# Sample states from two row groups of 32 tokens, state space states behind the first recurrence head, first evacuations on VectorE

## The chip, the cores and the metric

The kernel runs on one core of one Trainium2 chip. The metric is the time of one execution on the device in microseconds (us), as the median of several runs. In the profile the engines are called PE (TensorE, matrix products), DVE (VectorE), ACT (ScalarE), POOL (GpSimd) and SP (SyncE, which issues most DMA transfers).

## The reference

One inference step of a two-layer hybrid decoder. A prompt of 512 tokens and a sample group of 8 sequences of 8 tokens use the same weights; the model width is 1024. Layer 0 mixes tokens with 4 mLSTM heads and 4 retention heads, layer 1 with 4 HGRN2 heads (`hgrn`) and an S5 state space model. Behind each mixer come a squared-ReLU MLP and a gated per-layer embedding. Everything is fp32.

```python
# per layer i
hn = rmsnorm(h, norm_mix[i])
out, *st = ab_mixer(hn, ...) if i % 2 == 0 else cd_mixer(hn, ...)
h = h + out
hn = rmsnorm(h, norm_ff[i])
h = h + square(relu(hn @ w_ff1[i])) @ w_ff2[i]
gate = sigmoid(rmsnorm(h, norm_ple[i]) @ w_ple_gate[i])
h = h + gate * (p[i] @ w_ple_proj[i])
```

Each head of the three recurrences also returns its new state of 128 x 128 (mLSTM: 128 x 129 with the normaliser) for each of the 8 sample sequences, for instance for HGRN2:

```python
S = exp(b_last)[..., None] * S + einsum('bhsk,bhsv->bhkv', kc * exp(b_last[:, :, None] - b), vc)
```

Over the 64 sample tokens this is, for each sequence b, the product of the keys and the values of b's 8 tokens, added to the decayed old state.

## The kernel before

All 576 tokens (512 of the prompt, 64 samples) are one tile of 128 x 576. A projection is made a column at a time: 128 outputs by 576 tokens, from 8 blocks of 128 inputs. For fp32 accuracy weights and activations are split in a high and a low part, and a block is three products (`mm3`, L240 to L247), each in two halves of 288 tokens: 48 products on L245 for a column. The weight's high part is made by ACT (L233) and the low part by DVE or POOL (L234). A column collects in a buffer `pb` in PSUM, which an engine evacuates. Small products go to other PSUM buffers, `pm`. Where the pools are set by `psum(3)` there are three `pb` buffers and two `pm`; with `psum(2)` two and four.

The program runs `load` (the inputs, and the layer 0 embedding projection), the first mixer with mLSTM heads and retention heads, the MLP, the embedding, the second mixer, MLP, embedding, and the final norm. A scheduler sets each engine's order of instructions from the order of the program, a priority (`high_priority`) and the dependencies; an engine then runs its list strictly in that order, and so does SP with its DMAs.

Three places matter here.

`load` (L358 to L383). Two embedding tiles `pin` and the hidden state `h` of 8 tiles are loaded over SP, and eight columns of the embedding are computed. Each is evacuated to `po` with factor 0.5 by ACT (L380), and a DMA queue of POOL stores `po` to DRAM; `po` has three buffers. A copy of one column of `pin` to h[0] (L369) makes the load of h[0] wait until that copy is done, so SP issues it last of the eight.

`state_out` (L747 to L764) is called once for each of the 12 heads, for the sample sequences. POOL spreads the values of the 64 tokens to `Vm`, where the columns of sequence b keep only the rows of its tokens (a mask from `vmask`, L756), for three, three and two sequences. A PE product on L758 with the 64 tokens as its rows contracts the keys `Kt` with it, 384, 384 and 256 columns (387, 387 and 258 with the normaliser), and DVE adds each result to the state `s_in` (L761 or L763). The sample outputs of a head come from `s_in` and `qd` on L778 just before, in products that fill 32 columns of the PE array.

The second mixer (L1465 to L1490): four columns `su` of the state space model, then `s5_state` (L1203 to L1249) for four groups of channels `ct`: tables `sR` and `sE` from DRAM into five shared buffers, two groups of four products on L1220, and nine DVE instructions (L1226 to L1234, one of them a scan, L1230) that run the recurrence. Then `hgrn` (L1300) for heads 0 to 3, each with columns f, q, i and g (evacuations on L1313, L1334, L1337, L1340), a scan over tokens (L1329), exponent factors `e` (L1385, L1387) for a hierarchy of small products on PE (L1373, L1408), and its state. The outputs of the state space model are made after head 1.

Of the kernel before, what the change touches and what calls it, by code (L numbers as in the profile page):

```python
# [16 lines left out]
P = 128  # L17
NP = 512
NS = 64
# [28 lines left out]

def c0_layout():
    cols, n = {}, 0  # L50
    for name, w in (("ident", 128), ("qmask", 128), ("vmask", 8), ("m01", NT), ("negp", 128), ("negs", 64),
                    ("sel", 512), ("cos", NT), ("sin", NT), ("rdec", 512), ("rdecs", 256),
                    ("rint", 512), ("rints", 256), ("rkd", 4), ("rkds", 4)):
        cols[name] = (n, n + w)
        n += w
    return cols, n
# [7 lines left out]
def const0():  # L64
# [14 lines left out]
    qm = np.zeros((NB, NS), np.float32)  # L79
    qm[s // 8, s] = 1.0  # L80
    put("qmask", np.broadcast_to(qm[:4, :32].reshape(1, -1), (P, 128)))
    put("vmask", qm.T)
    sel = np.zeros((36, 4, P), np.float32)
    for h in range(4):
        sel[h, h] = 1.0
# [85 lines left out]
class K:  # L171
# [188 lines left out]
    def load(self):  # L360

        nc = self.nc
        with self.tc.tile_pool(name="lp", bufs=2) as lp:
            with self.tc.high_priority(60):
                raw = self.fetch("col2", "w_ple_proj", 0, 0, 0)
                pin = self.embed_in(0, lp, nc.sync)
                ws = [self.parts(raw)]

                nc.vector.tensor_copy(self.h[0][:, 0:1], pin[1][:, 0:1])  # L369
            for k in range(KD):  # L370
                nc.sync.dma_start(self.h[k], self.A["hT"][k])
                if k == 3:
                    ws.append(self.unit("col2", "w_ple_proj", 0, 512, 0))
            nc.sync.dma_start(self.cc, self.A["c0"][:, :NCC])
            for n2 in range(2):
                for n in range(4):
                    ps = self.cols(ws[n2], self.xple, (2 * n, 2 * n + 1))
                    o = lp.tile([P, NT], F32, name="po", tag="po", bufs=3)
                    with self.tc.high_priority(60):
                        nc.scalar.mul(self.sv(o), self.pv(ps), 0.5)  # L380
                    nc.gpsimd.dma_start(self.prd[n2 * 4 + n], o)
                if n2 == 0:
                    self.gate_w = self.unit("gate")  # L383
# [363 lines left out]
    def state_out(self, name, h, n, C, Kt, V, dec, hp):  # L747

        nc = self.nc
        Cn = C  # L750
        if dec is not None and not isinstance(dec, float):
            nc.gpsimd.tensor_tensor(Cn, C, dec.unsqueeze(2).to_broadcast([P, NB, n]), ALU.mult)
        for b0, b1 in ((0, 3), (3, 6), (6, 8)):
            ps = self.pmt()[:, :(b1 - b0) * n]
            Vm = hp.tile([NS, 3, n], F32, name="Vm", tag="Vm", bufs=2)[:, :b1 - b0]
            nc.gpsimd.tensor_tensor(Vm, V[:NS, 4, :n].unsqueeze(1).to_broadcast([NS, b1 - b0, n]),  # L756
                                    self.vmask[:, b0:b1].unsqueeze(2).to_broadcast([NS, b1 - b0, n]), ALU.mult)
            nc.tensor.matmul(ps, Kt[:NS, 4], Vm.rearrange("p b n -> p (b n)"), start=True, stop=True)  # L758
            o = Cn[:, b0:b1].rearrange("p b n -> p (b n)")
            if isinstance(dec, float):  # L760
                nc.vector.scalar_tensor_tensor(o, C[:, b0:b1].rearrange("p b n -> p (b n)"), dec, ps, ALU.mult, ALU.add)  # L761
            else:
                nc.vector.tensor_tensor(o, o, ps, ALU.add)  # L763
        nc.sync.dma_start(self.A[name][h], Cn)  # L764

    def qdiag(self, q, hp, tag="qd"):

# [694 lines left out]
    def mix1(self):  # L1462
        nc, tc = self.nc, self.tc
        with ExitStack() as st:
# [8 lines left out]
            with self.psum(3):  # L1473
                self.s5_in(xs, r, sp)
                r = r()
            st.enter_context(self.psum(2))
            self.s5_state(sp)
            self.hgrn(0, xs, r, hp)
            self.hgrn(1, xs, r, hp)
            self.s5_out(sp, range(4))  # L1480
            self.hgrn(2, xs, r, hp)
# [119 lines left out]
```

## Time and profile before

| | |
|---|---|
| median of 3 runs | 1675.05 us (1671.84 to 1675.14) |
| the profiled execution | 1673.67 us, span of the instructions 1671.9 us |
| PE busy | 1599.5 us, 96% of the span |
| DVE busy | 994.9 us, 60% |
| ACT busy | 619.5 us, 37% |
| POOL busy | 244.9 us, 15% |
| mean granted clock of PE | 0.979 |

The profile is of one execution. A busy time is the sum of an engine's instruction times, which can overlap with those of other engines; the span is from the first to the last instruction. The chain of waits follows the work that ended last back to what released it. The granted clock is a share of the full 2.4 GHz: 0.5 is the 1.2 GHz level, and a value between them is a mean over a stretch that has both.

### The profile page before, as it was taken

To read this page: it belongs to the slowest core of one execution; us is meant where nothing else is said; L and a number is where in the kernel's file an instruction comes from. 1 tells how busy PE (TensorE), PEld (TensorE's weight loads), DVE (VectorE), ACT (ScalarE), POOL (GpSimd) and SP (SyncE) were. 2 spreads that over 40 slices of the span, in tenths; PEclk is the share of its full clock that TensorE was granted. 3 is DMA by queue.
4 is the path that set the end of the run, shared out by engine and by line. 5 is a ranking of instruction groups with operands and counts; after the bars stand their busy time and mean duration, and the time that the engine had idled before them with its cause. 6 is when DMAs were issued, how large, how long until landed. Compare 5 with 4: busy or idle time off the path is not lost.

```text
span 1671.9 us, 30272 instructions
## 1 busy us (share of the span) xinstructions
PE 1599.5 (96%) x12613; PEld 1549.1 (93%) x12613; DVE 994.9 (60%) x1830; ACT 619.5 (37%) x1016; POOL 244.9 (15%) x236
## 2 busy tenths in 40 slices
PE   6999999999999999999999788989999999999996
PEld 6999799999999999999998778879999999999995
DVE  4987665658954636347666796386633424334365
ACT  5333222335313223144542356463522413224353
POOL 1321232301000000001023465241000000000100
PEclk8999999999999999999999889999999999999998
DMA  6322222223332323324436322522222222222221
GB/s 251 110 91 81 93 78 102 78 75 103 115 116 78 121 87 116 108 80 141 146 104 192 114 76 82 147 77 78 77 89 85 80 89 76 89 89 91 89 89 57
DMA packets 77226, 168.81 MB, mean 101 GB/s; under 512 B 29216, under 2 KB 34208, under 8 KB 76960
## 3 DMA queue, kind: packets, MB, share of 16 engines
q1 hardware_dynamic: 75432, 163.40, 28.9%
q8 instruction: 99, 1.62, 0.4%
q0 software_dynamic: 640, 2.36, 0.4%
q10 hardware_dynamic: 1016, 1.11, 0.2%
q14 instruction: 39, 0.32, 0.1%
HBM read 142.70 MB, written 24.13 MB: 100 GB/s over the span
## 4 chain that ended last, share of the span: by engine, by line
PE 85%; DVE 7%; ACT 3%; DMA 2%; issue 2%; SPq 1%; DVEq 0%; ACTq 0%
PE pb L245 77%; PE pm L758 2%; PE pm L528 1%; PE pm L778 1%; DVE e L1385 1%; PE pm L870 1%; SPq L1270 1%; DMA s5U<-yd 0%; SPq L1201 0%; ACT wh L233 0%; PE pm L795 0%; DVE s5w L1230 0%; ACT xh L280 0%; PE pm L872 0%; DVE h L429 0%
## 5 line engine op out<-in xcount | busy, mean ns | idle before, releaser
L245 PE MATMUL pb<-xh,wh 128*128 128x288 f32 x2480 | 548.6, 300 | 34.2 <-ACT po L380 7.2
L245 PE MATMUL pb<-xl,wh 128*128 128x288 f32 x2480 | 546.9, 299 | 0.0
L245 PE MATMUL pb<-xh,wl 128*128 128x288 f32 x2480 | 546.5, 299 | 0.0
L233 ACT CAST wh<-wr 128x1024 fp32r<-128x1024 f32 x219 | 229.7, 1049 | 745.2 <-PE pb L245 672.9
L245 PEld LDWEIGHTS pb<-xh,wh 128*128 128x128 f32 x2480 | 406.0, 191 | 44.1 <-issue 12.5
L245 PEld LDWEIGHTS pb<-xl,wh 128*128 128x128 f32 x2480 | 407.1, 191 | 5.7 <-issue 5.4
L245 PEld LDWEIGHTS pb<-xh,wl 128*128 128x128 f32 x2480 | 407.0, 191 | 4.0 <-issue 3.2
L234 DVE TENSOR_TENSOR wl<-wr,wh 128x1024 fp32r<-128x1024 f32 x199 | 246.2, 1238 | 24.6 <-ACT wh L233 16.0
L245 PE MATMUL pb<-uh,wl 128*128 128x288 f32 x1024 | 219.2, 296 | 0.0
L245 PE MATMUL pb<-ul,wh 128*128 128x288 f32 x1024 | 218.8, 295 | 0.0
L245 PE MATMUL pb<-uh,wh 128*128 128x288 f32 x1024 | 218.8, 295 | 0.0
L458 DVE TENSOR_TENSOR h<-h,pb 128x576 f32<-128x576 f32 x64 | 48.2, 754 | 210.8 <-PE pb L245 210.8
L245 PEld LDWEIGHTS pb<-uh,wl 128*128 128x128 f32 x1024 | 163.9, 188 | 0.6 <-DVE s5R L951 0.4
L245 PEld LDWEIGHTS pb<-uh,wh 128*128 128x128 f32 x1024 | 163.8, 188 | 0.6 <-issue 0.6
L245 PEld LDWEIGHTS pb<-ul,wh 128*128 128x128 f32 x1024 | 164.2, 188 | 0.0
L322 POOL TENSOR_TENSOR sqa<-sqa,sq 128x576 f32<-128x576 f32 x20 | 33.0, 1648 | 876.2 <-ACT sq L321 876.2
L445 DVE SCALAR_TENSOR_TENSOR fu<-pb,r 128x576 f32<-128x576 f32 x64 | 48.3, 756 | 179.4 <-PE pb L245 179.3
L234 POOL TENSOR_TENSOR wl<-wr,wh 128x1024 fp32r<-128x1024 f32 x20 | 50.8, 2543 | 103.6 <-ACT wh L233 102.0
L278 DVE TENSOR_TENSOR ul<-fu,uh 128x576 fp32r<-128x576 f32 x64 | 48.3, 755 | 9.5 <-ACT uh L277 9.3
L756 POOL TENSOR_TENSOR Vm<-V,cc 64x384 f32<-64x384 f32 (+3 forms) x36 | 32.0, 900 | 103.1 <-ACT V L740 63.8
L446 ACT ACTIVATE fu<-fu 128x576 f32<-128x576 f32 x64 | 43.8, 686 | 8.5 <-DVE fu L445 8.2
L281 DVE SCALAR_TENSOR_TENSOR xl<-h,vec,xh 128x576 fp32r<-128x576 f32 x48 | 39.7, 837 | 11.8 <-ACT xh L280 11.8
(459 smaller groups left out, 1506.9 us busy)
## 6 DMA issues: line engine op xcount, KB each, us to landing
wr<-in_w_dram SPq DMA_DIRECT2D x219, 512.0 KB, 3.2
sR<-Rd SPq DMA_DIRECT2D x12, 256.0 KB, 3.8
h<-in_hT_dram SPq DMA_DIRECT2D x8, 288.0 KB, 5.3
prd<-po POOLq DMA_DIRECT2D x8, 288.0 KB, 5.9
Gd<-s5G SPq DMA_DIRECT2D x4, 576.0 KB, 3.9
prj<-prd SPq DMA_DIRECT2D x8, 288.0 KB, 6.0
sG<-Gd SPq DMA_DIRECT2D x8, 288.0 KB, 5.0
s_in<-in_Cst_dram SPq DMA_DIRECT2D x4, 516.0 KB, 7.4
```

Of the source, the lines that this page charges most:

```text
L233: nc.scalar.copy(hi, raw)
L234: (nc.gpsimd if self.lo_pool else nc.vector).tensor_tensor(lo, raw, hi.bitcast(F32), ALU.subtract)
L245: mm(ps[:, j if bank is None else bank, :HALF], a, b[:, j * HALF:(j + 1) * HALF], start=first and a is wh and b is xh, stop=last and a is wl)
L278: nc.vector.tensor_tensor(lo, src, hi.bitcast(F32), ALU.subtract)
L281: nc.vector.scalar_tensor_tensor(lo, src, scale, hi.bitcast(F32), ALU.mult, ALU.subtract)
L322: (nc.vector if i or dve else nc.gpsimd).tensor_tensor(acc[i], acc[i], t, ALU.add)
L445: nc.vector.scalar_tensor_tensor(self.sv(u), self.pv(ps), 0.0, self.sv(r()), ALU.max, ALU.mult)
L446: nc.scalar.activation(u, u, AF.Square)
L458: nc.vector.tensor_tensor(self.sv(self.h[n]), self.sv(self.h[n]), self.pv(ps), ALU.add)
L528: nc.tensor.transpose(dst, src[:n, t0:t0 + tn], self.ident[:n, :n])
L756: nc.gpsimd.tensor_tensor(Vm, V[:NS, 4, :n].unsqueeze(1).to_broadcast([NS, b1 - b0, n]), self.vmask[:, b0:b1].unsqueeze(2).to_broadcast([N ...
L758: nc.tensor.matmul(ps, Kt[:NS, 4], Vm.rearrange("p b n -> p (b n)"), start=True, stop=True)
```

## The change

In `load` the copy to h[0] goes away, and the eight evacuations go from ACT to DVE. In `state_out` the 64 tokens are taken as two row groups, rows 0 to 31 with sequences 0 to 3 and rows 32 to 63 with sequences 4 to 7. A folded mask (four more columns of `vmask`) lets one POOL product serve both, with four blocks of 128 columns; two PE products follow, each with 32 rows and 512 columns, into two PSUM buffers. For mLSTM a third PE product with the mask itself as its 8 columns gives the normaliser. In the second mixer head 0 is called before `s5_state`.

```diff
@@ c0_layout
-    for name, w in (("ident", 128), ("qmask", 128), ("vmask", 8), ("m01", NT), ("negp", 128), ("negs", 64),
+    for name, w in (("ident", 128), ("qmask", 128), ("vmask", 12), ("m01", NT), ("negp", 128), ("negs", 64),
...
-    put("vmask", qm.T)
+    put("vmask", np.concatenate([qm.T, qm[:4].T + qm[4:].T], 1))
@@ load
-                pin = self.embed_in(0, lp, nc.sync)
+                self.embed_in(0, lp, nc.sync)
                 ws = [self.parts(raw)]
-
-                nc.vector.tensor_copy(self.h[0][:, 0:1], pin[1][:, 0:1])
...
-                        nc.scalar.mul(self.sv(o), self.pv(ps), 0.5)
+                        nc.vector.tensor_scalar(self.sv(o), self.pv(ps), 0.5, None, ALU.mult)
@@ state_out
-        Cn = C
-        if dec is not None and not isinstance(dec, float):
-            nc.gpsimd.tensor_tensor(Cn, C, dec.unsqueeze(2).to_broadcast([P, NB, n]), ALU.mult)
-        for b0, b1 in ((0, 3), (3, 6), (6, 8)):
-            ps = self.pmt()[:, :(b1 - b0) * n]
-            Vm = hp.tile([NS, 3, n], F32, name="Vm", tag="Vm", bufs=2)[:, :b1 - b0]
-            nc.gpsimd.tensor_tensor(Vm, V[:NS, 4, :n].unsqueeze(1).to_broadcast([NS, b1 - b0, n]),
-                                    self.vmask[:, b0:b1].unsqueeze(2).to_broadcast([NS, b1 - b0, n]), ALU.mult)
-            nc.tensor.matmul(ps, Kt[:NS, 4], Vm.rearrange("p b n -> p (b n)"), start=True, stop=True)
-            o = Cn[:, b0:b1].rearrange("p b n -> p (b n)")
...
+        Vm = hp.tile([NS, 4, P], F32, name="Vm", tag="Vm", bufs=2)
+        nc.gpsimd.tensor_tensor(Vm, V[:NS, 4, :P].unsqueeze(1).to_broadcast([NS, 4, P]),
+                                self.vmask[:, 8:].unsqueeze(2).to_broadcast([NS, 4, P]), ALU.mult)
+        ps = [self.pmt() for _ in range(2)]
+        rows = [slice(32 * g, 32 * g + 32) for g in range(2)]
+        for g in range(2):
+            nc.tensor.matmul(ps[g], Kt[rows[g], 4], Vm[rows[g]].rearrange("p b n -> p (b n)"), start=True, stop=True)
+        if n > P:
+            pn = self.pmt()[:, :8]
+            nc.tensor.matmul(pn, Kt[:NS, 4], self.vmask[:, :8], start=True, stop=True)
+        for g in range(2):
+            add(C[:, 4 * g:4 * g + 4, :P], ps[g].rearrange("p (b n) -> p b n", b=4))
+        if n > P:
+            add(C[:, :, P], pn)
@@ the second mixer
+            self.hgrn(0, xs, r, hp)
             self.s5_state(sp)
-            self.hgrn(0, xs, r, hp)
             self.hgrn(1, xs, r, hp)
```

The following rows are the instructions as they stand in an engine's list: line, operation, output and inputs with buffer numbers, shape, and how many stand together. First PE, before, at the state products of the first retention head (`s_in` and `qd` are the sample state and query, `pb` a projection column):

```order
L870 MATMUL pm_2588<-V_2537,W_2557 128x128
L872 MATMUL pm_2588<-Cs_2570,qi_2567 128x128
L778 MATMUL pm_2589<-s_in_2581,qd_2583 32x128 x8
L758 MATMUL pm_2608<-Vm_2609,Kt_2547 128x384
L758 MATMUL pm_2613<-Vm_2614,Kt_2547 128x384
L245 MATMUL pb_2664<-xl_368,wh_2660 128x288
```

The third product, L758 with 256 columns, stood 12 rows further down, between column products. The same place on PE after the change:

```order
L878 MATMUL pm_2571<-V_2520,W_2540 128x128
L880 MATMUL pm_2571<-Cs_2553,qi_2550 128x128
L786 MATMUL pm_2572<-s_in_2564,qd_2566 32x128 x8
L764 MATMUL pm_2593<-Vm_2591,Kt_2530 128x512
L764 MATMUL pm_2594<-Vm_2591,Kt_2530 128x512
L245 MATMUL pb_2640<-xl_367,wh_2636 128x288
```

Three products became two, which are neighbours here, and the third place among the columns is gone. Next DVE, before, at the start of the second mixer: the last evacuation of a state space column (`su`), the first channel group's recurrence (`s5w`, `s5Z`), and head 0's f column (`z`, from `pb_10000`):

```order
L1197 TENSOR_TENSOR su_9823<-pb_9774,r_9468 128x8x8
L1226 TENSOR_TENSOR s5w1_9869<-s5Z_9538,sR_9845 64x512
L1227 TENSOR_TENSOR s5w1_9869<-s5Z_9538,sR_9845 64x512
L1228 TENSOR_TENSOR s5w0_9868<-s5Z_9538,sR_9844 128x512
L1229 TENSOR_TENSOR s5w0_9868<-s5w0_9868,s5w1_9869 128x512
L1230 SCALAR_TENSOR_TENSOR s5w0_9868<-sR_9846,s5w0_9868 128x512
L1231 TENSOR_TENSOR s5w1_9869<-s5w0_9868,sR_9845 64x512
L1232 TENSOR_TENSOR s5w1_9869<-s5w0_9868,sR_9845 64x512
L1233 TENSOR_TENSOR s5w0_9868<-s5w0_9868,sR_9844 128x512
L1313 TENSOR_TENSOR z_10049<-pb_10000,r_9468 128x576
```

In the changed kernel DVE goes from the same evacuation to head 0, and its first recurrence instruction stands behind the second half of head 0's output `mo`, 76 instructions on:

```order
L1205 TENSOR_TENSOR su_9778<-pb_9729,r_9423 128x8x8
L1321 TENSOR_TENSOR z_9854<-pb_9805,r_9423 128x576
L1325 TENSOR_SCALAR z_9854<-z_9854 128x576
...
L809 SCALAR_TENSOR_TENSOR mo_10337<-pm_10331,gnh_82,gT_10042 128x64
L1234 TENSOR_TENSOR s5w1_10365<-s5Z_9493,sR_10341 64x512
L1235 TENSOR_TENSOR s5w1_10365<-s5Z_9493,sR_10341 64x512
```

The recurrence moved from ahead of head 0 to the middle of head 1. Further on in the same list, on DVE after the change, the fourth group's recurrence and head 2's f column (`z_11262`) stand among head 1's level work (`Wc`, `e`):

```order
L1236 TENSOR_TENSOR s5w0_10469<-s5Z_9493,sR_10445 128x512
L1321 TENSOR_TENSOR z_11262<-pb_11213,r_9423 128x576
L1237 TENSOR_TENSOR s5w0_10469<-s5w0_10469,s5w1_10470 128x512
L1384 COPY_PREDICATED Wc_10768<-lev_84,pm_10771 128x128
L1385 COPY_PREDICATED Wc_10768<-lev_84,pm_10771 64x32
L1393 TENSOR_TENSOR e_10891<-b_10560 128x144x2
L1238 SCALAR_TENSOR_TENSOR s5w0_10469<-sR_10447,s5w0_10469 128x512
```

Before, head 0's f column stood so among the first groups. In `load` DVE's list gains the evacuations `po`; after the change, from the split of h[3] to that of h[4] (`xl` is a low part, `sqa` the sum of squares of the norm):

```order
L281 SCALAR_TENSOR_TENSOR xl_348<-h3_124,vec_70,xh_347 128x576
L322 TENSOR_TENSOR sqa_326<-sqa_326,sq_351 128x576
L378 TENSOR_SCALAR po_184<-pb_171 128x576
L234 TENSOR_TENSOR wl_163<-wr1_160,wh_162 128x1024
L378 TENSOR_SCALAR po_200<-pb_187 128x576
L378 TENSOR_SCALAR po_216<-pb_203 128x576
L281 SCALAR_TENSOR_TENSOR xl_355<-h4_125,vec_70,xh_354 128x576
```

Here the first three evacuations stand between two splits; before, DVE ran the splits of h[2] to h[7] in a row with none between them.

## Rows read from the trace of the kernel before

**Rows 1.** The page, part 1: busy us of each engine (share) xinstructions.
```profile
PE 1599.5 (96%) x12613; PEld 1549.1 (93%) x12613; DVE 994.9 (60%) x1830; ACT 619.5 (37%) x1016; POOL 244.9 (15%) x236
```

**Rows 2.** The page, part 4: the chain that ended last, by engine, by line.
```profile
PE 85%; DVE 7%; ACT 3%; DMA 2%; issue 2%; SPq 1%; DVEq 0%; ACTq 0%
PE pb L245 77%; PE pm L758 2%; PE pm L528 1%; PE pm L778 1%; DVE e L1385 1%; PE pm L870 1%; SPq L1270 1%; DMA s5U<-yd 0%; SPq L1201 0%; ACT wh L233 0%; PE pm L795 0%; DVE s5w L1230 0%; ACT xh L280 0%; PE pm L872 0%; DVE h L429 0%
```

**Rows 3.** Busy time by stretch: us, busy by engine, PEclk, DMA share, GB/s.
```profile
350.00:840.00 490.00, 489.06 (x3694) 484.07 (x3694) 295.30 (x632) 173.02 (x240) 18.20 (x15) 1.00 0.33 109
892.00:1012.00 120.00, 101.05 (x1015) 94.40 (x1016) 95.47 (x127) 54.51 (x103) 60.22 (x47) 0.87 0.36 116
```

**Rows 4.** The same by stretch, of the column products on L245 alone.
```profile
350.00:840.00 490.00, 481.71 (x3585) 477.79 (x3585) 1.00 0.33 109
892.00:1012.00 120.00, 75.51 (x488) 72.35 (x489) 0.87 0.36 116
```

**Rows 5.** The same by stretch, of the recurrence's tile s5w alone (DVE).
```profile
892.00:1012.00 120.00, 38.99 (x36) 0.87 0.36 116
```

**Rows 6.** The same by stretch, of the state space products on L1220 alone.
```profile
892.00:1012.00 120.00, 9.25 (x64) 8.58 (x64) 0.87 0.36 116
```

**Rows 7.** PE's waits from 850 to 1180: us in total, times, longest.
```profile
PE pb L245 <- DVE z L1337: 6.3, 1, 6.3
PE pm L1220 <- DMA sE<-Ed: 6.3, 4, 3.2
PE pb L245 <- DVE gT L1340: 5.2, 1, 5.2
```

**Rows 8.** Timeline of DVE from 918 to 937: start, us, instruction.
```profile
927.52 3.25 DVE L1230 TENSOR_TENSOR_SCAN s5w<-sR,s5w 128x512 f32<-128x512 f32 x1
930.70 2.49 DVE L1387 TENSOR_TENSOR e<-e,q 128x256 f32<-128x256 f32 x1
933.11 0.74 DVE L1337 TENSOR_TENSOR z<-pb,r 128x576 f32<-128x576 f32 x1
...
934.21 0.69 DVE L1231 TENSOR_TENSOR s5w<-s5w,sR 64x512 f32<-64x512 f32 x1
```

**Rows 9.** Costliest groups, DVE from 892 to 1012: xcount | busy, mean ns.
```profile
L1230 DVE TENSOR_TENSOR_SCAN s5w<-sR,s5w 128x512 f32<-128x512 f32 x4 | 6.9, 1728 | 0.1
```

**Rows 10.** Busy time by stretch of 6 us, columns as in rows 3.
```profile
924.00:930.00 6.00, 3.70 (x28) 3.47 (x26) 5.90 (x4) 3.65 (x5) 6.00 (x4) 1.00 0.00 0
930.00:936.00 6.00, 1.30 (x4) 0.98 (x4) 5.92 (x8) 0.00 (x0) 2.90 (x1) 0.67 0.16 44
936.00:942.00 6.00, 3.55 (x16) 3.58 (x17) 3.39 (x7) 1.14 (x3) 0.00 (x0) 0.50 0.56 187
```

**Rows 11.** Timeline of PE from 234 to 241, the first retention head's state.
```profile
234.44 1.07 PE L778 MATMUL pm<-s_in,qd 128*32 128x128 f32 x16
235.44 1.55 PE L758 MATMUL pm<-Vm,Kt 64*128 64x384 f32 x4
236.93 0.40 PE L245 MATMUL pb<-xl,wh 128*128 128x288 f32 x1
...
239.78 0.70 PE L758 MATMUL pm<-Vm,Kt 64*128 64x256 f32 x2
240.41 0.40 PE L245 MATMUL pb<-xh,wl 128*128 128x288 f32 x1
```

**Rows 12.** Timeline of PE from 5 to 45, idle before and its releaser in brackets.
```profile
23.01 0.85 PE L245 MATMUL pb<-xh,wh 128*128 128x288 f32 x2 [5.04 <-ACT po L380]
30.63 0.59 PE L245 MATMUL pb<-xh,wh 128*128 128x288 f32 x2 [2.15 <-ACT po L380]
```

**Rows 13.** Timeline of DVE from 6 to 45, the splits of h.
```profile
17.37 4.46 DVE L281 SCALAR_TENSOR_TENSOR xl<-h,vec,xh 128x576 fp32r<-128x576 f32 x6
```

**Rows 14.** Timeline of ACT from 18 to 42, one of the eight evacuations.
```profile
27.79 0.65 ACT L380 ACTIVATE po<-pb 128x576 f32<-128x576 f32 x1 [2.62 <-DMA prd<-po]
```

**Rows 15.** The page, part 5: an evacuation of a column on DVE.
```profile
L445 DVE SCALAR_TENSOR_TENSOR fu<-pb,r 128x576 f32<-128x576 f32 x64 | 48.3, 756 | 179.4 <-PE pb L245 179.3
```

More of the change, by code (lines that the diff above doesn't have):

```diff
@@ L749, in state_out, with add @@
         nc = self.nc
-        Cn = C
-        if dec is not None and not isinstance(dec, float):
-            nc.gpsimd.tensor_tensor(Cn, C, dec.unsqueeze(2).to_broadcast([P, NB, n]), ALU.mult)
-        for b0, b1 in ((0, 3), (3, 6), (6, 8)):
-            ps = self.pmt()[:, :(b1 - b0) * n]
-            Vm = hp.tile([NS, 3, n], F32, name="Vm", tag="Vm", bufs=2)[:, :b1 - b0]
-            nc.gpsimd.tensor_tensor(Vm, V[:NS, 4, :n].unsqueeze(1).to_broadcast([NS, b1 - b0, n]),
-                                    self.vmask[:, b0:b1].unsqueeze(2).to_broadcast([NS, b1 - b0, n]), ALU.mult)
-            nc.tensor.matmul(ps, Kt[:NS, 4], Vm.rearrange("p b n -> p (b n)"), start=True, stop=True)
-            o = Cn[:, b0:b1].rearrange("p b n -> p (b n)")
+        if not isinstance(dec, float):
+            nc.gpsimd.tensor_tensor(C, C, dec.unsqueeze(2).to_broadcast([P, NB, n]), ALU.mult)
+        def add(o, ps):
             if isinstance(dec, float):
-                nc.vector.scalar_tensor_tensor(o, C[:, b0:b1].rearrange("p b n -> p (b n)"), dec, ps, ALU.mult, ALU.add)
+                nc.vector.scalar_tensor_tensor(o, o, dec, ps, ALU.mult, ALU.add)
             else:
                 nc.vector.tensor_tensor(o, o, ps, ALU.add)
-        nc.sync.dma_start(self.A[name][h], Cn)
+        Vm = hp.tile([NS, 4, P], F32, name="Vm", tag="Vm", bufs=2)
[12 more added lines that the diff above has]
+            add(C[:, :, P], pn)
+        nc.sync.dma_start(self.A[name][h], C)
     def qdiag(self, q, hp, tag="qd"):
```

## The prediction

> **What bounds the kernel now.** I read the page's busy table and chain first, then the busy time by stage, then the waits, and last the timelines of the stages that the change touches. PE is busy 1599.5 of 1671.9 us [rows 1], and the chain that ended last is PE for 85%, 77% of it the column products of L245 [rows 2]. So a saving counts only if it shortens PE's own work or an idle stretch of PE. The table by stage shows where PE is not full: from 350 to 840 us it is busy 489.06 of 490 at full clock, while from 892 to 1012, the start of the second mixer, it is busy 101.05 of 120 and the granted clock averages 0.87 [rows 3]. Here DVE is busy 95.47 of 120, and 38.99 of that are the 36 instructions of the state space recurrence [rows 3, 5]: nine for each of four groups of channels. In the waits of this stage PE's longest ends at z of head 0 (6.3 us) and another at gT (5.2) [rows 7]. DVE's timeline shows why: recurrence instructions, with a scan of 3.25 us, are queued ahead of z at 933.11, although the column of z was done by then [rows 8]. PE stood idle, the clock then fell to 0.67 and to 0.50 in the next slices [rows 10], that is partly and then wholly to the 1.2 GHz level after the idle time.
>
> The profiled execution took 1673.67 us, 1.8 more than its span, and the median of the runs is 1675.05. I make the sum as differences and take them from the median.
>
> **Part 1, state space behind head 0 (C).** First the present loss. Idle time is 120 - 101.05 = 18.95 us [rows 3]. The 488 column records took 75.51 us here, 0.1547 each, against 481.71/3585 = 0.1344 at full clock [rows 4]: 488 x 0.0203 = 9.9 us of slow clock. Together 28.9 us. The same slowdown on the small products of head 0 is not in it; with it the clock's share is at most 0.13 x 120 = 15.6, so 34.6 is the upper bound.
>
> In the new order PE goes from the state space columns straight to f, q, i and g of head 0, and DVE has z, the scan, e and gT of head 0 with no recurrence ahead of them. A column is 48 products of 0.1344 us, 6.45 us, so PE has 4 x 6.45 = 25.8 us, and part of head 1's first column, to cover head 0's chain on DVE. Some waits inside a head's levels (e, Wc, W) belong to any head and remain; I leave 5 us with their clock.
>
> The recurrence now stands behind mo of head 0. Its DVE work is unchanged: 39.0 us, plus three evacuations of about 0.75 us among it, about 41 us, before z of head 2, which holds a PSUM buffer. PE's cover there: the eight groups of L1220, 9.25 us [rows 6], and by the order the remaining 33 of 48 products of head 1's g column and three columns of head 2, 3.7 x 6.45 = 23.9, together 33 us. The shortfall is 41 - 33 = 8 us of idle, with the clock behind it (9.9 per 18.95 us of idle above, about half as much again) 12 us. If DVE runs the chain undisturbed it is much shorter: a 64x512 product of it takes 0.69 us at 934.21 [rows 8], where POOL has gone quiet [rows 10], so eight of the nine instructions at 0.69 and a scan at the mean of four, 1.73 [rows 9], make 7.25 a group, 29 in all, plus 2, which 33 us would cover: loss 0. POOL still makes the low parts of some weights in this stage, as it did beside the 3.25 us scan, when it was busy for 6.00 of 6 us [rows 10], so I stay nearer the contended end: 9 us. After: 5 + 9 = 14 us against 28.9, **C = 15 us**. Bounds: 28.9 - 27 = 2 if the stretch behind head 0 loses nearly as much as the present one, 34.6 - 5 = 29 if it loses nothing.
>
> A wait that moves: each group's tables arrive in five shared buffers, freed by the group before. PE waited 6.3 us in four such waits [rows 7]. They stay and are now queued in PE ahead of head 1's levels; that is in the 9. On SP the weight loads behind those table loads wait with them; the columns of head 2 are there by my walk. Head 2 onwards has the same order as before, so a lead gained here is kept.
>
> The Trainium skill (SBUF — State Buffer, "SBUF: two separate sides") says that a DVE instruction with two SBUF inputs and a GpSimd instruction that reads SBUF exclude each other for a whole instruction. The 3.25 us scan beside a busy POOL agrees [rows 8, 10]. By that rule the contended 41 us hold and C is 28.9 - 5 - 12 = 12; without it, 24.
>
> **Part 2, state products in two row groups (B).** In the first retention head two 384-column products take PE from 235.44 to 236.93, 1.48 us, and the third, of 256 columns among column products, from 239.78 to 240.41, 0.63 us [rows 11]. With a price a per column and s per entry into this shape, 768a + s = 1.48 and 256a + s = 0.63: a = 1.66 ns, s = 0.205 us. One 512-column product then costs 0.85. No trace of before has two row groups, so the pair is bounded: side by side 0.85 + 0.2 = 1.05, one after the other 1.70 + 0.2 = 1.90, against 2.11 now. The nearest row for the choice is that of the eight 128-column products (16 records) just before, which go to two column groups: 1.07 us [rows 11], less 0.2 for the entry 0.87, where one by one at 1.66 ns a column they would take 8 x 128 x 1.66 = 1.70. They overlap two deep, so I take 1.05.
>
> By the order the two products are neighbours in the last mLSTM head, all four retention heads and hgrn heads 0, 2 and 3; in mLSTM heads 0 to 2 and hgrn head 1 column products stand between them, since the second waits for a PSUM buffer that DVE frees. Retention: 4 x 1.06 = 4.2. Last mLSTM head: 1032a + s = 1.92 now, 1.05 after and up to 0.2 for the 8-column product of the normaliser, 0.7. Three hgrn heads: 3 x 1.06 = 3.2, but these lie in stretches where PE also waits, so 2.1. The four separated heads: mLSTM 2.33 now (1032a + 3s), then 2 x 1.05 + 0.22 = 2.32, nothing. **B = 7.0 us.** Bounds: serial, 8 x 0.2 = 1.6; another 0.2 at every one of the twelve heads for a switch between shapes, -1; everything in hgrn too, 9. POOL's product covers 512 columns instead of 1024 and DVE's two adds as many columns as the three before: both lie beside column products.
>
> The rows price the switch at 0.2 us. The Trainium skill (TensorEngine Tiling (Array Packing), "Key Properties") says that changing the tiling mode drains the TensorE, which speaks against the pair wherever full-height products stand on both sides. If a row-group mode cost one more such drain per head, B would be 7.0 - 12 x 0.2 = 4.6.
>
> **Part 3, start (A).** PE idles 5.04 us until 23.01 and 2.15 until 30.63, both ended by an evacuation on ACT [rows 12]. Eight of them at 0.65 us [rows 14], 5.2 us, leave ACT; on DVE an evacuation of this shape costs 0.756 [rows 15], 6.0 us. The first three now stand ahead of the last four splits of h (six splits took 4.46 us on DVE from 17.37 [rows 13]), which shortens the first idle time. But there are three buffers, and one evacuation waited 2.62 us for a transfer out [rows 14]; that remains, and PE's third start waits for the eighth, which now stands behind DVE's splits and sums. Dropping the copy puts h0 first on SP instead of last; the loads together end no sooner. I walk PE's restart to about 31 against 30.63: **A = +0.5 us** (-3 if the transfers out start earlier by what the first three gain, +2 if DVE's queue adds up).
>
> **Sum.** 1675.05 - 15 - 7.0 + 0.5 = 1653.6.
>
> **The rivals.**
> R1, the row groups don't overlap: B = 1.6, 1675.05 - 15 - 1.6 + 0.5 = 1659.0. For it: no trace shows two row groups. Against: the column groups of the row before.
> R2, the stall moves: the recurrence takes from head 1 nearly what it took from head 0, C = 3, 1675.05 - 3 - 7 + 0.5 = 1665.6. For it: DVE's 39 us are still there, one table transfer per group is waited for, and PE stops when both column buffers are full. Against: when the first chain starts, head 1's z, scan and first e work are already done on DVE, so there is less beside it than in head 0 now.
> R3, slower: head 1 pays more than head 0 did. The recurrence of 39 us and head 1's own evacuations and e work are one queue on DVE; its levels and z of head 2 stand between recurrence instructions. If PE stalls about 29 us there at half as much again for the clock, 43, plus 5 in head 0, the loss is 48 against 28.9 to 34.6: C = -13 at the worst, and with B at the serial 1.6 and A at +2 the time is 1675 + 13 - 1.6 + 2 = 1688; with B at 7 and C = -13 it is 1682. It decides where the loss passes 28.9 + 7 + 3.4 = 39 us.
> R4, the change does not do what it says: products that stand apart on PE gain nothing. The order shows four of twelve heads so, already in B; if all twelve came apart in time, B = 0: 1675.05 - 15 + 0.5 = 1660.6, within R1's chance.
>
> **How the numbers follow.** A measurement of this kernel can tell about 0.2%, 3.4 us, from no change. Forecast 0.50 (1643 to 1662 with its own bounds), R1 0.15, R2 0.22, R3 0.13. Faster: 0.50 + 0.15 + 0.17 of R2 = 0.82; same: 0.05 of R2 and 0.03 of R3 = 0.08; slower: 0.10. Predicted 1653.6. The range runs from 1640 (C 25, B 9, A -1) to 1671 (C near 2, B at 3), which leaves about 0.06 below and 0.14 above.
>
> **What would show it.** In the profile of the changed kernel: the waits on z and gT of head 0 gone and the columns of head 0 without a gap; the recurrence after mo of head 0, with PE waiting on its tables or on z of head 2 for less than 10 us; the retention pairs at 1.05 us from their start to the next column product (1.9 would be R1); PE's third start at 30 to 32 us. I am wrong if PE's idle time between the state space columns and the levels of head 2 is not smaller than now, or if the pair takes 1.9.

## The result and the profile after

The changed kernel takes 1688.8 us in the median (1687.5 to 1691.1 in four runs) against 1673.6 for the kernel before in the same runs: a ratio of 1.0092, interval 1.0074 to 1.0111. It is slower by about 15 us, where about 21 us faster was forecast. The busy table and the chain of waits after, from the page:

```profile
PE 1606.6 (95%) x12597; PEld 1558.2 (92%) x12597; DVE 1000.6 (59%) x1829; ACT 609.1 (36%) x1004; POOL 225.8 (13%) x212
...
PE 82%; DVE 10%; ACT 3%; issue 2%; DMA 1%; SPq 1%; POOL 0%; DVEq 0%; ACTq 0%
```

PE has fewer instructions than in [rows 1] and is busy longer, a first sign of a slower clock; on the chain DVE has 10% where it had 7% [rows 2].

Where did the time go? Both kernels run the same 10512 column products of L245 in the trace, so the start of the n-th of them can be compared. The table gives, in us, how much later (+) or earlier (-) it starts than in the trace of before. e1, e2, e5 and e6 are experiments described below: all but the moved recurrence, the moved recurrence alone, the start alone, the state products alone.

| n | start before | place | after | e1 | e2 | e5 | e6 |
|---|---|---|---|---|---|---|---|
| 200 | 46.5 | behind `load` | -3.0 | -2.1 | 0.5 | -3.0 | 0.8 |
| 1200 | 245.3 | in the first retention head | -1.3 | -2.0 | 0.6 | -3.0 | -0.3 |
| 1800 | 355.6 | behind the last retention head | -3.2 | -4.0 | 0.6 | -3.0 | -2.3 |
| 5200 | 820.5 | ahead of the second mixer | -4.3 | -5.1 | 0.6 | -3.0 | -3.3 |
| 6200 | 1012.0 | at head 1 | -19.0 | -9.2 | -22.1 | -4.3 | -6.2 |
| 6600 | 1120.0 | at head 2 | 20.3 | -8.1 | 18.9 | -3.4 | -5.5 |
| 10400 | 1637.2 | end | 17.5 | -9.1 | 16.9 | -4.8 | -6.5 |

Up to the second mixer the change leads by 4.3 us. At head 1 it leads by 19.0, though part of that is work put off: the recurrence's own products have not come yet. Then 39 us are given back within 400 column products. To set like beside like, here is the stretch from the 5200th column product to the 7000th, which holds the same work: before, after, and e1, which is the changed kernel without the moved recurrence (us, busy of PE, PEld, DVE, ACT, POOL, then PEclk, DMA share, GB/s):

```profile
820.50:1188.40 367.90, 329.57 (x3172) 312.31 (x3171) 259.91 (x406) 179.66 (x325) 134.16 (x104) 0.94 0.34 108
816.20:1204.40 388.20, 340.40 (x3165) 324.19 (x3164) 261.26 (x402) 173.81 (x321) 125.73 (x96) 0.90 0.32 103
815.50:1177.80 362.30, 326.13 (x3164) 310.95 (x3164) 254.26 (x402) 177.20 (x323) 125.53 (x96) 0.94 0.34 110
```

After against before, the stretch is 20.3 us longer. PE idles 9.5 us more (47.8 instead of 38.3), and it is busy 10.8 us more with no more work, at a mean granted clock of 0.90 instead of 0.94. So the slower clock costs about as much as the idle time itself. The changed kernel's stretch in pieces of 24 us, with the same columns:

```profile
888.00:912.00 24.00, 22.41 (x166) 22.20 (x167) 13.86 (x18) 9.07 (x13) 9.84 (x5) 1.00 0.51 149
912.00:936.00 24.00, 20.87 (x355) 19.96 (x353) 15.74 (x26) 14.76 (x29) 15.21 (x15) 0.93 0.15 49
936.00:960.00 24.00, 17.09 (x121) 15.33 (x120) 21.22 (x36) 14.13 (x29) 14.27 (x13) 0.84 0.24 88
960.00:984.00 24.00, 24.00 (x153) 23.61 (x153) 14.30 (x15) 4.39 (x11) 5.80 (x4) 0.80 0.41 131
984.00:1008.00 24.00, 12.94 (x80) 12.49 (x78) 16.27 (x17) 3.01 (x6) 5.72 (x2) 0.84 0.32 106
...
1056.00:1080.00 24.00, 24.00 (x128) 24.00 (x128) 4.47 (x4) 3.31 (x7) 2.36 (x1) 0.60 0.46 131
```

Head 0's columns and levels, the first two rows, run with 4.7 us of idle time in 48. Then PE idles, most of all from 984 to 1008, and between and after the idle times it runs for long at the lower clock. PE's waits from 885 to 1170 name three places:

```profile
PE pm L803 <- DVE hs L799: 9.9, 2, 6.6
PE pm L1228 <- DMA sE<-Ed: 7.4, 1, 7.4
PE pb L245 <- DVE q L1342: 5.5, 2, 5.1
```

The waits of [rows 7] on z and gT of head 0 are gone, and these stand in their place.

**The wait on the tables.** DVE's timeline of the changed kernel (start, us, instruction, idle before in brackets) shows the recurrence of the four groups:

```profile
965.49 0.69 DVE L1234 TENSOR_TENSOR s5w<-s5Z,sR 64x512 f32<-64x512 f32 x1 [3.74 <-ACT s5Z L1229]
...
980.07 2.72 DVE L1234 TENSOR_TENSOR s5w<-s5Z,sR 64x512 f32<-64x512 f32 x1 [3.73 <-ACT s5Z L1229]
...
987.65 2.71 DVE L1241 TENSOR_TENSOR s5w<-s5w,sR 128x512 f32<-128x512 f32 x1
990.29 0.75 DVE L1342 SCALAR_TENSOR_TENSOR q<-pb,r 128x576 f32<-128x576 f32 x1
...
998.88 0.69 DVE L1234 TENSOR_TENSOR s5w<-s5Z,sR 64x512 f32<-64x512 f32 x1 [7.25 <-ACT s5Z L1229]
...
1006.48 0.69 DVE L1241 TENSOR_TENSOR s5w<-s5w,sR 128x512 f32<-128x512 f32 x1
```

and SP's queue, SP's own waits from 995 to 1012 (us, times, longest) and PE in the same kernel show what DVE and PE wait for:

```profile
997.58 5.75 SPq L1220 DMA_DIRECT2D sR<-Rd  x3
1006.47 1.05 SPq L1224 DMA_DIRECT2D sE<-Ed  x2
```

```profile
SPq L1220 <- DVE s5w L1238: 4.1, 1, 4.1
SPq L1224 <- DVE s5w L1240: 3.1, 1, 3.1
SPq L1224 <- DVE s5w L1241: 0.4, 1, 0.4
```

```profile
991.18 0.82 PE L245 MATMUL pb<-xh,wh 128*128 128x288 f32 x2 [5.14 <-DVE q L1342]
996.36 2.08 PE L1228 MATMUL pm<-s5U,sE 128*128 128x72 f32 x16
1009.50 2.80 PE L1228 MATMUL pm<-s5U,sE 128*128 128x72 f32 x12 [7.43 <-DMA sE<-Ed]
```

It is a loop. The next group's three sR come first on SP and take the buffers that are free first: two of the products' tables and the one that the scan L1238 has read. The two sE, behind them, take the last two, which the recurrence of the group before frees with L1240 and L1241; the first is issued at 1006.47, as L1240 ends. PE's products wait for sE, ACT's copies to s5Z for these, and DVE for ACT. So DVE, the engine with too much to do by the prediction, stands idle for 3.74, 3.73 and 7.25 us ahead of three of the four groups, and PE meanwhile is stopped at 991 by a column buffer whose evacuation `q` stands behind the recurrence in DVE's list.

**The wait on hs.** The normalisation of head 0's output is a string of instructions of 128 x 5 on DVE, and PE stands at L803 until its product `hs`. From the same DVE timeline, and POOL's:

```profile
950.64 2.26 DVE L287 SCALAR_TENSOR_TENSOR st<-st 128x5 f32<-128x5 f32 x1
...
955.18 0.15 DVE L287 SCALAR_TENSOR_TENSOR st<-st 128x5 f32<-128x5 f32 x1
...
956.62 0.89 DVE L799 TENSOR_TENSOR hs<-hs,st 128x512 f32<-128x512 f32 x2
```

```profile
950.53 2.34 POOL L234 TENSOR_TENSOR wl<-wr,wh 128x1024 fp32r<-128x1024 f32 x1
```

The same instruction takes 0.15 us at 955.18 and 2.26 beside POOL's low part of a weight: from 950.64 to 952.90, while POOL runs from 950.53 to 952.87. The Trainium skill (SBUF — State Buffer, "SBUF: two separate sides") says the later of two such instructions blocks until the first has finished; this row agrees.

**The clock.** The last row of the stretches has PE busy for 24.00 of 24 us at 0.60. It is the output products of the state space model; PE's groups of them from 880 to 1180 (xcount | busy us, mean ns | idle before), before and then after, where their lines are L1273 and L1274:

```profile
L1265 PE MATMUL pm<-s5U,sT 128*128 128x72 f32 x64 | 12.3, 277 | 0.0
L1266 PE MATMUL pm<-s5Z,sG 128*128 128x72 f32 x64 | 12.2, 272 | 0.0
```

```profile
L1273 PE MATMUL pm<-s5U,sT 128*128 128x72 f32 x64 | 17.7, 378 | 0.0
L1274 PE MATMUL pm<-s5Z,sG 128*128 128x72 f32 x64 | 17.5, 371 | 0.0
```

The same products take 10.7 us more. PE had idled 3.3 us for hs of head 1 (the rest of the 9.9), until 1050.9, and from 1051.3 to 1075.2 the granted clock was 0.50 with PE busy all the time:

```profile
1051.30:1075.20 23.90, 23.90 (x111) 23.52 (x110) 1.86 (x4) 2.61 (x6) 1.22 (x2) 0.50 0.44 136
```

### The profile page after: what moved, and what is told of

Read it like the earlier page. It is cut to its first block, busy times and chain, and to the rows that moved or that the text cites. A ratio compares the mean times of both kernels' runs of the same rounds, so it can differ in the third digit from the quotient of the medians.

```text
span 1689.4 us, 30207 instructions
## 1 busy us (share of the span) xinstructions
PE 1606.6 (95%) x12597; PEld 1558.2 (92%) x12597; DVE 1000.6 (59%) x1829; ACT 609.1 (36%) x1004; POOL 225.8 (13%) x212
## 4 chain that ended last, share of the span: by engine, by line
PE 82%; DVE 10%; ACT 3%; issue 2%; DMA 1%; SPq 1%; POOL 0%; DVEq 0%; ACTq 0%
PE pb L245 74%; DVE e L1395 1%; PE pm L526 1%; PE pm L1273 1%; PE pm L1274 1%; PE pm L1228 1%; SPq L1209 1%; DVE e L1393 1%; DVE st L287 1%; PE pm L786 1%; PE pm L764 1%; PE pm L803 1%; PE pm L878 1%; ACT hsq L795 1%; ACT wh L233 0%
## 5 line engine op out<-in xcount | busy, mean ns | idle before, releaser
L245 PE MATMUL pb<-xh,wh 128*128 128x288 f32 x2480 | 550.1, 301 | 35.2 <-ACT xh L277 6.2
L245 PE MATMUL pb<-xh,wl 128*128 128x288 f32 x2480 | 545.6, 299 | 1.4 <-POOL wl L234 1.4
L245 PE MATMUL pb<-xl,wh 128*128 128x288 f32 x2480 | 546.3, 299 | 0.0
L245 PEld LDWEIGHTS pb<-xh,wh 128*128 128x128 f32 x2480 | 406.8, 192 | 45.2 <-issue 14.0
L245 PEld LDWEIGHTS pb<-xl,wh 128*128 128x128 f32 x2480 | 407.0, 191 | 6.1 <-issue 5.7
L245 PEld LDWEIGHTS pb<-xh,wl 128*128 128x128 f32 x2480 | 406.6, 191 | 4.4 <-issue 2.0
L245 PE MATMUL pb<-uh,wl 128*128 128x288 f32 x1024 | 219.1, 296 | 0.0
L245 PE MATMUL pb<-ul,wh 128*128 128x288 f32 x1024 | 218.8, 295 | 0.0
L245 PE MATMUL pb<-uh,wh 128*128 128x288 f32 x1024 | 218.6, 295 | 0.0
L245 PEld LDWEIGHTS pb<-uh,wl 128*128 128x128 f32 x1024 | 163.9, 188 | 0.6 <-DVE s5R L959 0.4
L245 PEld LDWEIGHTS pb<-uh,wh 128*128 128x128 f32 x1024 | 163.9, 188 | 0.6 <-issue 0.6
L245 PEld LDWEIGHTS pb<-ul,wh 128*128 128x128 f32 x1024 | 164.1, 188 | 0.0
L280 ACT ACTIVATE xh<-h,vec 128x576 fp32r<-128x576 f32 x48 | 37.0, 774 | 29.1 <-DVE h L514 17.4
```

Of the source, the lines that this page charges most:

```text
L245: mm(ps[:, j if bank is None else bank, :HALF], a, b[:, j * HALF:(j + 1) * HALF], start=first and a is wh and b is xh, stop=last and a is wl)
L280: nc.scalar.mul(hi, src, scale)
```

## The experiments

**e1 and e2: is it the moved recurrence?** e1 is the changed kernel with `s5_state` ahead of head 0 again; e2 is the kernel before with only that call moved.

```diff
-            self.hgrn(0, xs, r, hp)
             self.s5_state(sp)
+            self.hgrn(0, xs, r, hp)
```

> The changed kernel with s5_state put back ahead of head 0; the start and the state products stay changed. Theory 1 (the move of s5_state costs about 20 us, the start gives 3.0 and the state products of layer 0 about 1.3): 1673.6 - 3.0 - 1.3 and up to 3 more from the hgrn heads, 1666 to 1670, with the lead of 4.3 us at the end of layer 0 kept to the end. Theory 2 (the state products, which now want two PSUM buffers at once, upset the hgrn heads, and the place of s5_state does not matter): 1684 to 1690.

> The kernel before with only s5_state moved behind head 0. Theory 1: 1673.6 + 20 = 1690 to 1695. Theory 2 (the state products do the harm): 1660 to 1675.

Measured: e1 1664.5 us, ratio to before 0.9948 (0.9933 to 0.9963); e2 1687.6, ratio 1.0081 (1.0065 to 1.0097). Theory 1 holds: the moved recurrence alone turns a gain into a loss. It costs 13.8 us alone and 24.3 on top of the other two parts (1688.8 - 1664.5). Most of the difference is in the output products: in e2's trace PE waits only 0.6 us for hs ahead of them, and they take 26.3 us instead of 35.2. e2 also meets the tables, in its worst wait:

```profile
1009.87 2.38 PE L1220 MATMUL pm<-s5U,sE 128*128 128x72 f32 x10 [9.90 <-DMA sE<-Ed]
```

**e3 and e4: the table loop.** In `s5_state` the two sE of a group are taken and loaded ahead of the three sR. The sE of a group then no longer get the buffers that the recurrence just before them frees last. e3 is the changed kernel with this, e4 is e1 with it.

```diff
+            Es = [sp.tile([P, 4, P], F32, name="sE", tag="sE", bufs=SEB) for _ in range(2)]
+            for q, E in enumerate(Es):
+                nc.sync.dma_start(E.rearrange("p g n -> p (g n)"), self.Ed[ct][:, 512 * q:512 * q + 512])
             R = [sp.tile([P, 512], F32, name="sR", tag="sE", bufs=SEB) for _ in range(3)]
...
-                E = sp.tile([P, 4, P], F32, name="sE", tag="sE", bufs=SEB)
-                nc.sync.dma_start(E.rearrange("p g n -> p (g n)"), self.Ed[ct][:, 512 * q:512 * q + 512])
+                E = Es[q]
```

> The changed kernel, in s5_state the two tables sE of a group are loaded ahead of the three sR instead of behind them, so that the next group's sE take the buffers that PE frees first and need not wait for DVE's recurrence. Theory 1a (PE, ACT, DVE and the tables form a loop: a group's products wait for tables, these for the recurrence of the group before, this for ACT and PE): the wait of 7.4 us of the state space products on sE goes, DVE's idle 3.7, 3.7 and 7.3 us ahead of the groups shrink, time 1689 - 10 to 20 = 1669 to 1679. Theory 1b (DVE's work of 39 us is simply too much for head 1): no change, 1686 to 1690.

> e1 with the tables sE loaded ahead of sR as well. Theory 1a: four waits of 6.3 us in all on sE at the head of the mixer become less than 2, with their slow clock 5 to 8 us less than e1, 1659 to 1664. Theory 1b: as e1, since z and gT of head 0 still stand behind the recurrence on DVE, within 2 us of it.

Measured: e3 1668.4 us, ratio 0.9976 (0.9960 to 0.9991), so 20.4 us better than the changed kernel; e4 1664.3, ratio 0.9945 (0.9925 to 0.9964), no different from e1. Theory 1a holds for the moved recurrence: an edit that takes no work from DVE removes most of the loss, so the sum of DVE's work was not by itself what cost it. DVE's groups from 885 to 1180 show the loop open, the changed kernel first, then e3 (the last field is the idle time before):

```profile
L1234 DVE TENSOR_TENSOR s5w<-s5Z,sR 64x512 f32<-64x512 f32 x4 | 4.8, 1195 | 20.4 <-ACT s5Z L1229 20.4
```

```profile
L1236 DVE TENSOR_TENSOR s5w<-s5Z,sR 64x512 f32<-64x512 f32 x4 | 2.8, 702 | 2.7 <-ACT s5Z L1231 2.5
```

In e3 the tables of the fourth group are issued before the recurrence of the third starts (SP's queue and DVE's timeline); in the changed kernel they are issued as it ends:

```profile
984.44 1.05 SPq L1220 DMA_DIRECT2D sE<-Ed  x2
985.96 0.69 DVE L1236 TENSOR_TENSOR s5w<-s5Z,sR 64x512 f32<-64x512 f32 x1
```

PE's waits on sE fall from 7.4 to 2.8 us. Not all of the 20.4 us is the loop itself: in e3 PE no longer idles for hs of head 1, and the output products, which took 35.2 us, take 24.5 again. That is about half of the gain, and it came by way of the clock.

For e4 1a was wrong: ahead of head 0 the same edit gains nothing that the runs can tell. In its trace PE still waits 5.7 us for sE, and 12.8 for hs.

**e5 and e6: the other two parts alone**, each put on the kernel before: e5 the hunks of `load`, e6 those of `state_out` and its mask.

> The kernel before with the start alone changed (copy to h[0] gone, evacuations on DVE). Theory 1: column products run about 3.0 us earlier from 45 us on, and this lead is partly lost at the last mLSTM head, where PE waits for DVE anyway; 1670 to 1673 in the median. Theory 2 (the lead of 3 us at the start is lost in later waits altogether): within 0.5 us of the kernel before.

> The kernel before with the state products alone changed. Theory 1: a lead of 0 until the last mLSTM head, about 0.65 us for each of the four retention heads, near 2 to 3 at the end of layer 0, and 3 to 5 more in the hgrn heads, so that with e5 it adds up to e1: 1667 to 1670. Theory 2 (only 0.65 a head wherever it is used): 1670 to 1672.

Measured: e5 1667.0 us, ratio 0.9955 (0.9941 to 0.9970); e6 1666.1, ratio 0.9949 (0.9932 to 0.9967). Both are a little better than expected. In the medians they don't add: 7.1 and 8.1 us apart, 9.3 together in e1, a shortfall of 5.9 us where the three intervals together leave open about 4.6. In the table of starts the two leads add up to the second mixer within about a microsecond (-3.0 and -3.3 apart; -5.1 in e1) and fall short within it; what takes the rest there is not settled.

**e7 and e8: DVE beside POOL.** `LOP = "fqig"` lists the columns of a head whose low parts POOL makes. With `LOP = ""` DVE makes them, 16 units more. e7 is the changed kernel with this, e8 is e4 with it.

```diff
-LOP = "fqig"
+LOP = ""
```

> The changed kernel with the low parts of the 16 hgrn weight units made by DVE (1.23 us each, 20 us in all) instead of POOL (2.5 us each). Theory 3 (DVE instructions that stand still beside POOL, such as 2.26 us for a 128x5 instruction beside a low part of 2.34, make the 6.9 us wait on head 0's normalisation and lengthen the loop): the tiny instructions take 0.17, the wait on hs is under 3 us, time 1675 to 1684. Rival (DVE's total work decides): 20 us more on DVE cost 5 to 20 us, 1692 to 1708.

> e4 with those low parts on DVE. Theory 3: e4's waits on hs (12.8 us) fall below 5, time 1654 to 1661. Rival (DVE's total work decides): DVE is already busy for 95 of 120 us at the head of this mixer, 1668 to 1680.

Measured: e7 1668.5 us, ratio 0.9972 (0.9957 to 0.9987), 20.3 better than the changed kernel; e8 1649.8, ratio 0.9853 (0.9836 to 0.9869), 14.6 better than e4. Theory 3's direction holds, with more gain than expected, and the waits that it named shrank: PE's waits for hs fall from 9.9 to 2.7 us in e7 and from 12.8 to none in e8. The busy time of the tile s5w on DVE from 885 to 1180, changed kernel and then e7 (with PEclk, DMA share, GB/s):

```profile
885.00:1180.00 295.00, 36.64 (x36) 0.87 0.31 97
```

```profile
885.00:1180.00 295.00, 28.43 (x36) 0.94 0.33 105
```

and DVE's groups of the low parts and of L287 there, in the same order:

```profile
L234 DVE TENSOR_TENSOR wl<-wr,wh 128x1024 fp32r<-128x1024 f32 x9 | 11.0, 1220 | 0.6 <-issue 0.4
...
L287 DVE SCALAR_TENSOR_TENSOR st<-st 128x5 f32<-128x5 f32 x12 | 4.1, 339 | 0.3
```

```profile
L234 DVE TENSOR_TENSOR wl<-wr,wh 128x1024 fp32r<-128x1024 f32 x28 | 35.9, 1284 | 6.2 <-ACT wh L233 5.7
...
L287 DVE SCALAR_TENSOR_TENSOR st<-st 128x5 f32<-128x5 f32 x12 | 2.0, 164 | 0.3
```

DVE does 24.9 us more of low parts, and yet the recurrence takes 8.2 us less, a tiny instruction half, and the granted clock rises from 0.87 to 0.94. What counted as busy on DVE was in part standing still.

How much of the 20.3 us that standing still is worth is not separated. The edit also makes each of the 16 low parts sooner (1.2 us on DVE, 2.5 on POOL) and clears POOL's list for its other work, such as its half of the factors `e`. PE's direct waits on a low part of POOL were 1.4 us in the changed kernel, so that much of the rival is small; the rest of it no run tests. And as in e3, the output products take 24.5 us again instead of 35.2, although PE's waits on sE even grow, from 7.4 to 9.7 us.

**e9 to e11: do the two costs add up, and does it pay elsewhere?** e9 is the changed kernel with both edits; e10 the kernel before with `LOP = ""` alone; e11 is e1 with it.

> The changed kernel with both the tables loaded first (e3) and the low parts on DVE (e7). Theory 4 (two separate costs: the table loop and DVE standing still beside POOL): the gains of e3 and e7 add up at least in part, and with both gone the place of s5_state no longer hurts: within 4 us of e8, 1646 to 1654. Theory 5 (e3 and e7 each remove the same thing, the length of the loop): no better than either alone, 1664 to 1670, and the place ahead of head 0 (e8) stays 15 us or more better.

> The kernel before with only the low parts on DVE. Theory 3 (DVE standing still beside POOL costs time whatever the rest): the 6.3 us wait on z of head 0 and 5.2 on gT shrink, 12 to 18 us faster than before, 1656 to 1662. Rival (it pays only in the changed kernel): within 4 us of before.

> e1 with the low parts on DVE, tables in the old order. Theory 3: most of e8's gain over e4 is the low parts' alone, 1650 to 1654. Rival (tables first and low parts are needed together): 1658 to 1664.

Measured: e9 1657.1 us, ratio 0.9906 (0.9884 to 0.9929); e10 1657.2, ratio 0.9912 (0.9885 to 0.9940); e11 1653.2, ratio 0.9885 (0.9862 to 0.9909). Theory 3 holds in all places: 16 us on the kernel before, 11.3 on e1. Of theories 4 and 5 neither holds whole. The gains of e3 and e7 add up in part, 31.7 us together against 20.4 and 20.3. They overlap by 9.0 us, and the 10.7 us of the slowed output products, which either edit alone gives back, would account for that. But the place ahead of head 0 stays better by 7.3 us, not by 15 and not by less than 4. The four variants by place of the recurrence, medians in us; by the intervals of the runs each cost in the last column is uncertain by 4 us or more, so 4.1 and 7.3 can't be told apart:

| with the other two parts, and | ahead of head 0 | behind head 0 | cost of the move |
|---|---|---|---|
| nothing else | 1664.5 (e1) | 1688.8 (after) | 24.3 |
| tables first | 1664.3 (e4) | 1668.4 (e3) | 4.1 |
| low parts on DVE | 1653.2 (e11) | 1668.5 (e7) | 15.3 |
| both | 1649.8 (e8) | 1657.1 (e9) | 7.3 |

**e12: half the recurrence behind head 0.** e8 with groups 0 and 1 ahead of head 0 and groups 2 and 3 behind it.

```diff
...
-            self.s5_state(sp)
+            self.s5_state(sp, (0, 1), False)
             self.hgrn(0, xs, r, hp)
+            self.s5_state(sp, (2, 3), True)
```

> e8 with the state space states of channel groups 0 and 1 ahead of head 0 and those of groups 2 and 3 behind it. Theory 6 (with loop and contention gone, DVE's queue ahead of head 0 still costs e8 something, and half of it can go behind head 0 without the price of the whole): 1644 to 1649, faster than e8. Rival (whatever part of the recurrence stands behind head 0 takes columns from head 1 and 2 that their levels need as cover): between e8 and e9, 1650 to 1657.

Measured: 1657.4 us, ratio 0.9903 (0.9881 to 0.9925). Theory 6's gain did not come: half costs as much time as all. The rival's time came, a little above its end, but its mechanism is not what the traces show. 5950 column products stand ahead of head 0's levels in e8 and 5926 in e9; between the levels of heads 2 and 3 there are 174 in e8 and 125 in e9. So e9 has 49 products, 6.6 us at 0.1344 us each, less to put beside head 2's levels. But e11, with the recurrence ahead of head 0, has 125 there too and takes 1653.2, and e12 has 210.

What e12 lost is seen in its trace, which is 12 us longer than e8's. PE waits 7.4 us for hs of head 1, the output products of the state space model follow directly, and the granted clock is 0.50 from 1010.3 to 1037.6:

```profile
1010.30:1037.60 27.30, 23.92 (x108) 23.50 (x109) 6.92 (x21) 2.69 (x7) 0.69 (x2) 0.50 0.53 163
```

These products take 34.4 us in e12 and 24.5 in e8. It is the changed kernel's wait for hs and slow stretch again; why hs came late in e12 is not shown. For e9 no such place is found: from the 5200th to the 7000th column product it falls 11.5 us behind e8, with 5.2 us more idle time of PE and up to 7 us of clock, in several smaller waits. What costs that is open.

## Why the prediction was wrong, point by point

**Part 1 (C = +15 us) was wrong in sign**: -13.8 alone, -24.3 with the rest. The step that failed is "the shortfall is 41 - 33 = 8 us of idle". It compared how much DVE has to do with how much PE has, as if both could always work. The term ahead of it was a little short: head 0 without the recurrence lost 4.7 us of idle time and at most 1.7 of clock from 888 to 936, where 5 together was put, and the 6.6 us in which PE waits for head 0's own hs come behind that and had no term. Behind head 0 the four groups are a chain through DVE, SP, ACT and PE that has its own length. DVE idles 20.4 us in it, PE 5.1 us for q and 7.4 for the tables. Two sentences of the prediction touch this and were not followed: "each group's tables arrive in five shared buffers, freed by the group before", which was put into the 9 us without a price of its own, and "on SP the weight loads behind those table loads wait with them", where the point was that the products' own tables wait for the buffers that the recurrence frees last. e3 shows it: the order of five loads is worth 20.4 us, about half of it by way of the clock of the output products. The prediction's own sign of being wrong came too: from the last evacuation of a state space column to head 2's levels PE idles 30.8 us (889.2 to 1092.6), where it idled 26.2 before (892.6 to 1078.2).

**The clock was undersized.** "About half as much again" as the idle time came from [rows 3, 4], from column products alone. After, in the two 24 us stretches from 960 to 984 and 1056 to 1080 PE is busy without a break and loses 0.20 x 24 and 0.40 x 24, 14.4 us together, to the clock. A wait of 3.3 us was followed by 10.7 us on products that ran at the full clock before. From the 5200th to the 7000th column product it took 10.8 us beside 9.5 of idle time, where the prediction put it at half the idle time.

**POOL was seen and priced too low.** The prediction took the contended 3.25 us scan [rows 8] as a reason to stay "nearer the contended end" of DVE's 39 us, and the recurrence did take 36.64 in the changed kernel. In e7 it took 28.43, near the 29 that the prediction worked out for an undisturbed DVE. What it missed is that the same thing strikes instructions of 128 x 5 on which PE waits, and that taking 16 low parts off POOL is worth 16 us to the kernel before (e10). The conditional sum, C = 12, counted only DVE's total and so missed it too.

**Part 2 (B = 7.0 us) was right in total, in part by luck**: 8.1 in e6. By the table of starts e6 gains 4.1 us up to the second mixer (from 0.8 to -3.3), where the prediction put 4.9. The 3.2 us after that come with up to 5 us less lost to the clock in the second mixer, for which it had no term, while PE idles 2.8 us more there. The row groups run side by side. The changed kernel's pair in the first retention head, from PE's timeline, to set beside [rows 11]:

```profile
234.35 1.07 PE L786 MATMUL pm<-s_in,qd 128*32 128x128 f32 x16
235.35 1.13 PE L764 MATMUL pm<-Vm,Kt 32*128 32x512 f32 x4
```

From 235.35 to the next column product at 236.41 it is 1.06 us, where 1.05 was put and R1 asked for 1.9. The Trainium skill (TensorE: Matmul & The Clock Gate, "Part 3: Packing small matmuls") says that row groups run concurrently with starts about 4 ns apart; here the two products' first records start at 235.352 and 235.359. The Trainium skill (TensorEngine Tiling (Array Packing), "Key Properties") says that changing the tiling mode drains the TensorE. One more such drain in each head, which would have made B 4.6, does not show: nothing is paid beyond the 0.2 us already in s. The sizes inside were off: the first three retention heads gained about 0.65 us each, not 1.06, because PE then reached the head's output product earlier and waited for DVE there (from the start of the last column product to that of L803 the traces have 0.14 us before and 0.66 after).

**Part 3 (A = +0.5 us) was wrong in sign too**, by 3.5 us: -3.0 at the 200th product and -7.1 in e5's median. PE's waits in `load` after:

```profile
13.92 0.53 PE L245 MATMUL pb<-xh,wh 128*128 128x288 f32 x2 [0.87 <-DVE po L378]
23.19 0.50 PE L245 MATMUL pb<-xh,wh 128*128 128x288 f32 x2 [3.97 <-DVE po L378]
29.08 0.51 PE L245 MATMUL pb<-xh,wh 128*128 128x288 f32 x2 [0.94 <-ACT wh L233]
```

and the first 42 us by stretch, before and then after (columns as in [rows 3]):

```profile
0.00:42.00 42.00, 28.62 (x170) 28.15 (x171) 20.88 (x34) 24.06 (x36) 6.69 (x19) 0.88 0.68 250
```

```profile
0.00:42.00 42.00, 30.00 (x194) 29.16 (x195) 28.33 (x46) 19.49 (x28) 6.71 (x19) 0.96 0.70 262
```

The failed step is "I walk PE's restart to about 31". The waits on evacuations and weights sum to 5.8 us instead of 7.2 [rows 12], the third start is at 29.08, and with shorter waits the granted clock was 0.96 instead of 0.88, which is 0.08 x 42 = 3.4 us of clock at most; the prediction had no term for that. The bound of -3 had the right size and not the right reason: the first three transfers out did not start earlier, but from 14.2 us on instead of 13.1 (POOL's queue). They landed sooner, 3.1 us after their issue in the median of the eight instead of 5.9, and no evacuation waited for one, where one had waited 2.62 us [rows 14]. Why they landed sooner is not shown.

**The rivals.** R3, slower, with 0.13, is what happened, and 1688.8 lies just above its 1682 to 1688. Its sum is not sound: it takes the loss of 48 from the larger present loss, 34.6; from 28.9 it would be C = -19, not "-13 at the worst", and with B at 7 and A at 0.5 about 1688. Its point of decision, 39 us of loss, was passed: 28.9 + 13.8 = 42.7 by e2. But its mechanism, one queue of work on DVE, is not the one that the runs showed; e3 contradicts it. R1 and R4 did not happen.

## What to carry to other kernels

Where work is moved behind other work, follow its whole chain round all engines and queues once (who frees the buffers of the next round, and what is queued ahead of that load), since comparing two engines' sums of work misses a loop in which both wait. Look at what order the loads of a round stand in a shared set of buffers: here putting the loads of the next round's first step first was worth 20 us where the chain was on PE's path, and nothing where it was not (e4). Add the clock to the price of a wait, and look at what PE does right behind it. An operation on POOL beside a busy DVE is not free even when POOL has time: moving 16 of them to DVE gave DVE more work, and all five variants of this kernel that tried it were 11 to 20 us faster; the fastest, e8 at 1649.8 us, is 1.5% faster than the kernel before.

## What the runs showed of the hardware that I had not expected

A DVE instruction of 128 x 5 took 2.26 us instead of 0.15 to 0.17 beside a POOL instruction of 2.34 us, ending 0.03 us after it. fp32 products in two row groups of 32 ran wholly side by side, 1.06 us for a pair of 512 columns where a single one was worked out at 0.85, with 0.2 more for the entry. And PE stayed at the 1.2 GHz level for 24 us, from 1051.3 to 1075.2, while it was busy without a gap, mostly with 72-column products; before, without the wait of 3.3 us ahead of them, the same products ran at 2.4 GHz. In e12 the same happened behind a wait of 7.4 us. In e4 a wait of 6.6 us for the same hs ended at 1021.6, but there PE had 2.6 us of column products to do first; the clock was back at 1.00 at 1024.6, before the 72-column products began at 1025.2, and they ran at full clock. Three cases are no rule; in these the price of the wait went with what PE did right behind it.
